# One encoder block on one core: the recurrent output projection made from seven combined products, and modulation rows moved between stages

## The chip, the cores and the metric

The kernel runs on one core of one Trainium2 chip. The metric is device time of one execution in microseconds (us); lower is better. The core has a matrix engine (TensorE, PE in the profile), three engines for elementwise work (VectorE or DVE, ScalarE or ACT, GpSimd or POOL), and SyncE (SP), whose queue issues nearly all DMAs here. Each engine works through its own list of instructions.

## The reference, cut to what matters

One layer of a hybrid encoder on x of 1024 tokens by 1024 channels, all in float32. The part that the change rewrites is the recurrent branch of the mixer.

```python
x = sandwich(x, ffn1, ..., 0.5)       # FFN 1
x = sandwich(x, mix,  ..., 1.0)       # mixer
x = sandwich(x, ffn2, ..., 0.5)       # FFN 2

mod = silu(c) @ w_ada + b_ada         # 9 rows of 1024: shift, scale, gate of each sub-layer

def mixer(h, ...):
    q, k, v, xr, yr, g_att, g_rec = split(h @ w_in)
    att = chunked_attention(q, k, v, rel_bias) @ w_att_o
    rec = (rg_lru(conv(xr), ...) * gelu(yr)) @ w_rec_o
    merged = sigmoid(g_att) * att + sigmoid(g_rec) * rec
    return merged @ w_out
```

## The kernel before, in words

**Numbers as two parts.** TensorE multiplies a rounded form of float32. So each operand X is cut into a high part (a CAST by ScalarE, L147) and a low part (X minus the high part, a subtraction by VectorE or GpSimd, L148), and each product is three matmuls: high by high, high by low, low by high. The helper `split` records both cuts, `prep` loads a weight tile into the pool of raw tiles (tag `raw`, three buffers) and cuts it, and `mm3` (L494 to L496) issues the three matmuls. A matmul has a 128x128 stationary operand and a moving one of 128x512.

**Stages, in order of time.** FFN 1, the recurrence with its input projections (`lru_phase`), the recurrent output (`rec_out_phase`), attention (`att_phase`), the merge of both branches (`merge_phase`), the output projection (`out_phase`), FFN 2. In FFN 1 and FFN 2 and in the output projection, 2x2 blocks of operands are already multiplied in seven combined products where eight would be the plain way: some products use sums of blocks of weights and of activations. An FFN's up half goes in 22 blocks of columns; blocks 4 to 21 of FFN 1 (3 to 21 of FFN 2) use seven products (L716 to L718), with the weight sums made by GpSimd one block ahead (`mix`, L694), and GpSimd also makes the sums for the down half (`all_sums`, L914). The down half is a list of units, one per product and pair of row blocks, each of 12 matmuls (L976).

**The recurrence.** For each of eight channel blocks b: projections, a convolution, two gates, then `scan`: ScalarE makes exponent, tanh, square and root (L1183 to L1187), GpSimd one product (L1189), VectorE the scan (L1190) and its product with the gelu branch (L1191, tile `a`). The result is cut at once into `rh` (ScalarE, L1193) and `rl` (VectorE, L1194).

**The recurrent output.** For each of eight channel blocks n: 48 matmuls make the gate (`gr` weights; ScalarE takes tanh, L1257), 48 matmuls make the output block (`ro` weights by `rh`, `rl`), VectorE multiplies both (L1269), and a DMA stores the block to `part` (L1270). Gate n+1 is placed ahead of output n. Two side tasks run beside this. `out_weights` loads `w_out`, makes the weight blocks and sums of the seven products of the output projection, cuts them (`wo`) and stores 28 tiles of 512 KB to `outw` in DRAM; the output projection loads them again (`wu`). And `bgq`, a queue of generators for modulation rows, is stepped by `bg`.

**Modulation rows.** `ada_acc` (L202 to L207) loads eight tiles of `w_ada` of 512 KB (`rawa`) and adds them up on VectorE with the weights `c_act`: one plain product and seven SCALAR_TENSOR_TENSOR on 128x1024. `ada_cols` turns the sum into columns (scale and shift), `ada_gate` into a gate row. Their number v is 3 for shift, 4 for scale and 5 for gate of the mixer, 6, 7 and 8 of FFN 2. Before, 2 (gate of FFN 1), 3 and 4 are worked off in FFN 1; 6, 7, 5 and 8 in the recurrent output. Gates 5 and 8 go to DRAM and are loaded later (`load_gate`). In the up half of FFN 1, hooks after products call first the constants of the recurrence (`early`), then `bg`: one hook per block, after product 3, with the `w_ada` tile in the temporary pool `u`. In the down half `bg` is called once per unit of the first three products.

**Order.** Inside FFNs, the output projection and (after the change) the new products, the order of each engine's instructions is as written (`manual_schedule`); elsewhere a scheduler orders them, and it may move later instructions of other generators in between. SP issues its DMAs in order; one that waits for a free buffer holds those behind it.

Of the kernel before, what the change touches and what calls it, by code (L numbers as in the profile page):

```python
# [23 lines left out]
P = 128  # L24
# [24 lines left out]
def kernel(  # L49
# [239 lines left out]
    gate_d = {sub: dpool.tile([P, D], F32, name=f"gate{sub}") for sub in (1, 2)}  # L289
# [224 lines left out]
    def ffn(sub, w_gu, w_down, hh, hl, xin, xout):  # L514
# [266 lines left out]
        def up_phase(started):  # L781
# [291 lines left out]

    C_Q, C_K, C_V, C_XR, C_YR, C_GA, C_GR = 0, 512, 1024, 1536, 2560, 3584, 4608
# [37 lines left out]

    def lru_phase(hh, hl, tail):
        rec_h, rec_l = [], []
# [64 lines left out]
        def scan(b, st):  # L1179
# [12 lines left out]
            rh, rl = t4("rh", F32R), t4("rl", F32R)  # L1192
            nc.scalar.copy(rh, a)  # L1193
            nc.vector.tensor_tensor(rl, a, rh.bitcast(F32), op=ALU.subtract)  # L1194
            rec_h.append(rh)
            rec_l.append(rl)
# [24 lines left out]
        def rest():  # L1221
            for kind, part in (("x", xr_part), ("y", yr_part)):
# [15 lines left out]
            return rec_h, rec_l, wts  # L1238
# [3 lines left out]
    def rec_specs():  # L1242
        specs = {}
        for n in range(KB + 1):
            if n < KB:
                specs["gr", n] = partial(prep_cols, w_in, C_GR + n * P)
            if n > 0:
                specs["ro", n - 1] = partial(prep_cols, w_rec_o[0], (n - 1) * P)
        for n in ("q", "k"):
            specs[n, 0] = partial(prep_cols, w_in, (C_Q if n == "q" else C_K))  # L1250
        return specs

    def rec_out_phase(hh, hl, rec_h, rec_l, wts, part, others):
        def gate(n):
            tg = tu("tg")
            for sh, pj in enumerate(proj(wts["gr", n], hh, hl)):
                nc.scalar.activation(tg[:, sh * 512 : (sh + 1) * 512], pj, AF.Tanh, scale=0.5)  # L1257
            return tg

        nxt = gate(0)  # L1260
        for n in range(KB):
            tg = nxt
            if n + 1 < KB:
                nxt = gate(n + 1)
            bg(4)
            pr = proj(wts["ro", n], rec_h, rec_l)
            for sh in range(2):
                sl = slice(sh * 512, (sh + 1) * 512)
                nc.vector.scalar_tensor_tensor(tg[:, sl], tg[:, sl], 1.0, pr[sh], op0=ALU.add, op1=ALU.mult)  # L1269
            nc.sync.dma_start(part[n * P : (n + 1) * P, :], tg)  # L1270
            for _ in range(4):
                bg()
                next(others, None)
        bg_flush()
        assert next(others, None) is None
# [285 lines left out]
    H1, H2 = slice(0, 512), slice(512, 1024)  # L1561

    def pair_steps(weights, top, bot):

        t1, t2, b1, b2 = top[:, H1], top[:, H2], bot[:, H1], bot[:, H2]
        add, sub_ = ALU.add, ALU.subtract
        if weights:
            return (t1, t2, t1, sub_), (t2, b2, t2, sub_), (b2, b2, t1, sub_), (b1, b1, b2, sub_)
        return (b2, t2, b2, add), (t2, t1, t2, sub_), (t1, b2, t1, sub_), (b1, b1, t1, sub_)

    OUT_PAIRS = KB // 2
    OUT_STREAM = (1, 2, 6, 5, 3, 7, 4)
    out_w = {
        (p, j): dpool.tile([P, 2, 512], F32, name=f"outw{p}_{j}") for p in OUT_STREAM for j in range(OUT_PAIRS)
# [555 lines left out]
```

## Time and profile before

| what | value |
|---|---|
| median of 3 runs | 2180.91 us (2178.07 to 2181.05) |
| the profiled execution | 2171.58 us |
| its span, first to last instruction | 2169.7 us |
| mean granted TensorE clock | 0.998 |
| matmul instructions | 9925 |
| recurrent output: first and last start of a matmul on `rh` | 912.4 and 1071.6 us |
| bytes moved by DMA | 383.55 MB |

Spans of instructions come from the profiled execution. A row of the timeline gives start, duration, engine, line of the kernel, operation, output and inputs, and in brackets how long the engine had been idle and what ended that. A row by groups gives the number of instructions, busy time and mean nanoseconds of one. A row by windows gives the busy time of PE, PEld, DVE, ACT and POOL in a stretch, each with its count, then the granted clock, the busy share of the DMA engines and GB/s.

### The profile page before, as it was taken

The page shows a single profiled execution, that of the slowest core. Times are in us where ns is not written, and L with a number is a line of the kernel's source. Part 1 is how long each engine was busy: PE and PEld are TensorE (multiplying, and loading weights), DVE is VectorE, ACT ScalarE, POOL GpSimd, SP SyncE. Part 2 cuts the span into 40 slices and gives each one's busy share as a digit, 9 for nine tenths or more (in the row PEclk, how much of TensorE's full clock was granted, in tenths as well). Part 3 has the DMA queues.
Part 4 walks back from the last instruction along what each step waited for, and adds up shares of the span by engine and source line. Part 5 has one row for each costly group of instructions (what it writes and reads, how often), then busy time and mean ns, then how long its engine had stood idle before and what let it go on. Part 6 is the DMA issues. An engine that isn't in the chain of part 4 may idle for free.

```text
span 2169.7 us, 26880 instructions
## 1 busy us (share of the span) xinstructions
PE 2130.5 (98%) x9925; PEld 1767.7 (81%) x9925; DVE 1335.1 (62%) x1796; ACT 1025.5 (47%) x1619; POOL 665.3 (31%) x498
## 2 busy tenths in 40 slices
PE   7999999999999999999999999999999999999998
PEld 5888788888878888888798988888888888888877
DVE  7755676567457777675436665576676564543466
ACT  5433333334447787722147777436443333334443
POOL 1168885431104011000021120002078883422102
PEclk9999999999999999999999999999999999999999
DMA  9356774368575111299812013467157653347365
GB/s 327 105 190 242 242 259 156 123 234 314 185 246 194 44 48 43 89 326 325 270 40 71 26 52 99 158 215 262 64 199 278 243 206 107 126 148 276 120 231 186
DMA packets 266364, 383.55 MB, mean 177 GB/s; under 512 B 17488, under 2 KB 171256, under 8 KB 266232
## 3 DMA queue, kind: packets, MB, share of 16 engines
q1 hardware_dynamic: 253312, 335.60, 46.3%
q10 hardware_dynamic: 12920, 46.23, 5.5%
q8 instruction: 78, 1.28, 0.2%
q14 instruction: 54, 0.44, 0.1%
HBM read 275.86 MB, written 109.05 MB: 177 GB/s over the span
## 4 chain that ended last, share of the span: by engine, by line
PE 82%; DVE 6%; DMA 6%; ACT 4%; issue 1%; SPq 1%; POOL 0%; POOLq 0%; DVEq 0%; ACTq 0%
PE px L976 8%; PE pv L976 7%; PE pj L494 7%; PE pj L495 7%; PE pj L496 7%; PE psX L716 6%; PE psX L718 6%; PE psX L717 6%; PE pj L1330 6%; PE psZ L716 3%; PE psZ L718 3%; PE psZ L717 3%; PE px L1667 2%; DMA rawd<-downs 2%; PE pv L1377 2%; PE pv L1667 2%
## 5 line engine op out<-in xcount | busy, mean ns | idle before, releaser
L147 ACT CAST dh<-rawd 128x1024 fp32r<-128x1024 f32 x154 | 161.1, 1053 | 207.2 <-PE pv L976 66.5
L148 DVE TENSOR_TENSOR dh<-rawd,dh 128x1024 fp32r<-128x1024 f32 x130 | 161.6, 1247 | 149.7 <-ACT dh L147 141.7
L707 DVE TENSOR_TENSOR wm<-raw,wm 128x512 fp32r<-128x512 f32 x152 | 159.9, 1055 | 151.1 <-ACT wm L706 145.9
L494 PE MATMUL pj<-hh,wh 128*128 128x512 f32 x562 | 221.1, 394 | 0.0
L495 PE MATMUL pj<-hl,wh 128*128 128x512 f32 x562 | 219.1, 390 | 1.1 <-DVE hl L357 1.1
L496 PE MATMUL pj<-hh,wl 128*128 128x512 f32 x562 | 219.1, 390 | 0.0
L976 PE MATMUL px<-dh,dh 128*128 128x512 f32 x608 | 187.5, 389 | 1.2 <-DVE dh L148 1.2
L976 PE MATMUL pv<-dh,dh 128*128 128x512 f32 x528 | 163.3, 390 | 3.3 <-DVE dh L148 3.3
L148 POOL TENSOR_TENSOR wl<-raw,wh 128x1024 fp32r<-128x1024 f32 x20 | 48.3, 2421 | 314.3 <-ACT wh L147 269.8
L976 PE MATMUL px<-dh 128*128 128x512 f32 x352 | 137.4, 390 | 0.0
L914 POOL TENSOR_TENSOR act<-act,act 128x512 f32<-128x512 f32 x54 | 85.4, 1582 | 168.3 <-DMA act<-act 109.8
L976 PEld LDWEIGHTS px<-dh,dh 128*128 128x128 f32 x608 | 113.9, 188 | 25.6 <-DVE dh L148 2.1
L495 PEld LDWEIGHTS pj<-hl,wh 128*128 128x128 f32 x562 | 105.6, 188 | 22.9 <-DVE hl L357 1.9
L496 PEld LDWEIGHTS pj<-hh,wl 128*128 128x128 f32 x562 | 105.5, 188 | 22.0
L494 PEld LDWEIGHTS pj<-hh,wh 128*128 128x128 f32 x562 | 105.5, 188 | 21.5 <-DVE a L529 0.3
L976 PEld LDWEIGHTS pv<-dh,dh 128*128 128x128 f32 x528 | 98.7, 188 | 25.6 <-DVE dh L148 5.5
L716 PE MATMUL psX<-hh,wm 128*128 128x512 f32 x296 | 115.4, 390 | 1.3 <-ACT mixes L739 1.1
L716 PE MATMUL psX<-hs,wm 128*128 128x512 f32 x296 | 115.6, 390 | 0.1
L717 PE MATMUL psX<-hl,wm 128*128 128x512 f32 x296 | 115.2, 389 | 0.0
L718 PE MATMUL psX<-hs,wm 128*128 128x512 f32 x296 | 115.2, 389 | 0.0
L717 PE MATMUL psX<-hs,wm 128*128 128x512 f32 x296 | 115.2, 389 | 0.0
L718 PE MATMUL psX<-hh,wm 128*128 128x512 f32 x296 | 115.1, 389 | 0.0
(345 smaller groups left out, 5487.0 us busy)
## 6 DMA issues: line engine op xcount, KB each, us to landing
rawa<-in_w_ada_dram SPq DMA_DIRECT2D x56, 512.0 KB, 5.5
rawd<-acts SPq DMA_DIRECT2D x88, 256.0 KB, 3.9
rawd<-downs SPq DMA_DIRECT2D x88, 256.0 KB, 4.4
raw<-in_w_in_dram SPq DMA_DIRECT2D x44, 512.0 KB, 3.7
raw<-in_ffn_w_gu_dram SPq DMA_DIRECT2D x43, 512.0 KB, 4.8
sr<-in_ffn_w_gu_dram SPq DMA_DIRECT2D x39, 512.0 KB, 6.0
act<-act SPq DMA_DIRECT2D x37, 512.0 KB, 5.0
acts<-act ACTq DMA_DIRECT2D x36, 512.0 KB, 4.1
```

The costliest lines, as they stand in the source:

```text
L147: nc.scalar.copy(hi, raw)
L148: (eng or nc.vector).tensor_tensor(lo, raw, hi.bitcast(F32), op=ALU.subtract)
L494: nc.tensor.matmul(dst, wh[:, kk, :], xhk[:, sl], start=first, stop=False)
L495: nc.tensor.matmul(dst, wh[:, kk, :], xlk[:, sl], start=False, stop=False)
L496: nc.tensor.matmul(dst, wl[:, kk, :], xhk[:, sl], start=False, stop=last)
L707: nc.vector.tensor_tensor(t[:, 1], src, t[:, 0].bitcast(F32), op=ALU.subtract)
L716: nc.tensor.matmul(dst, t[:, 0, kk, :], xh, start=first and kk == 0, stop=False, skip_group_check=True)
L717: nc.tensor.matmul(dst, t[:, 0, kk, :], xl, start=False, stop=False, skip_group_check=True)
L718: nc.tensor.matmul(dst, t[:, 1, kk, :], xh, start=False, stop=last and kk == 3, skip_group_check=True)
L976: nc.tensor.matmul(dst, a_[:, 0, tk], w_[:, 1, :], start=first and n == 0, stop=last and n == 2, skip_group_check=True,)
L1330: nc.tensor.matmul(d, a[:, k, :], b[k][:, sl], start=k == 0 and i == 0, stop=k == KB - 1 and i == 2)
L1667: nc.tensor.matmul(dst, a[:, s, tk], w[:, t, :], start=first and n == 0, stop=last and n == 2, skip_group_check=True)
```

## The change

**Seven products for the recurrent output.** The 1024x1024 product of `w_rec_o` (transposed) by the recurrent rows is done in 28 units: seven products p in the order 1, 2, 6, 5, 3, 7, 4, each over four pairs j of row blocks, 12 matmuls a unit. `RecOperands` holds the operands: `load` brings one raw weight tile of 128x512 per unit (from `w_rec_o` for p = 1, 2, 4, from a new DRAM tensor `recs` that holds sums for p = 6, 5, 3, 7), `cut` cuts weight and activation two units ahead, `sums` makes the activation sums in place. Results of 128x512 are copied and added into `ys`. The tiles `rh` and `rl` are gone: `a` is kept whole and cut unit by unit. `rec_sums` makes the sums of `w_rec_o` in float32 during the recurrence: per pair two loads, four subtractions or additions on VectorE, two stores.

**Gates.** Gates 0 and 1 come ahead of the 28 units, gates 2 to 7 behind them; the product with the gate is one instruction of 128x1024 (L1368 of the new kernel).

**Output projection.** `weight_sums` stores only products 3 to 7 (20 tiles); the blocks for products 1 and 2 are loaded plain from `w_out` at the end of the merge and cut there and in the output projection (`cut_w`).

**Modulation rows.** Rows 6 and 7 move to FFN 1, whose up half now has two hooks per block (after products 6 and 3), with the `w_ada` tile in the `raw` pool; row 8 moves to the down half of FFN 2 and no longer goes through DRAM; row 5 stays beside the recurrent output.

The diff, cut to its core:

```diff
@@ ada_acc
-            elif raw_home[0] == "u":
-                raw = tu("rawa")
@@ up_phase
-                    if i == 3:
+                    if i in (6, 3):
                         if next(early, BANK) is BANK and sub == 0:
-                            raw_home[0] = "u"
                             bg(1)
-                            raw_home[0] = "raw"
+    def rec_sums():
+        for j in range(OUT_PAIRS):
+            pair = [t4("rtop"), t4("rbot")]
+            rows = [slice((2 * j + i) * P, (2 * j + i + 1) * P) for i in range(2)]
+            for t, r in zip(pair, rows):
+                nc.sync.dma_start(t, w_rec_o[0, r, :])
+            yield
+            for o, a, b, op in pair_steps(False, *pair):
+                nc.vector.tensor_tensor(o, a, b, op=op)
+            for t, r in zip(pair, rows):
+                nc.sync.dma_start(rec_s[r, :], t)
+            yield
@@ scan
-            rh, rl = t4("rh", F32R), t4("rl", F32R)
-            nc.scalar.copy(rh, a)
-            nc.vector.tensor_tensor(rl, a, rh.bitcast(F32), op=ALU.subtract)
+            rec.append(a)
@@ rec_out_phase
+        gate(0, wts)
+        bg(2)
+        gate(1, wts)
+        bg(2)
+        ops.load(2)
...
+            ops.cut(2)
+            for p in OUT_STREAM:
+                if p in (1, 6, 7, 4):
+                    dst = chain
+                elif p != 3:
+                    dst = [bank("pv") for _ in range(half)]
+                for j in range(OUT_PAIRS):
+                    n = ops.order.index((p, j)) + 1
+                    ops.load(n + 3)
+                    for i in range(half):
+                        mm(dst[i], i, p, j, j == 0 and p in (1, 2, 5), j == OUT_PAIRS - 1)
+                    ops.cut(n + 2)
+                    if p == 1:
+                        ops.keep(3, j, t4("keep", F32R, (P, 2, 512)))
+                        ops.sums(j, 0)
+                    elif p == 2:
+                        ops.sums(j, 1)
+                    elif p == 4:
+                        next(others, None)
+                    elif j == 1:
+                        bg(1, False)
+                    if p == 7 and j < 2:
+                        gated(j)
@@ main
-        bgq.extend([ada_gate(0, 0.5), ada_cols(3), ada_cols(4)])
+        bgq.extend([ada_gate(0, 0.5)] + [ada_cols(v) for v in (3, 4, 6, 7)])
-        bgq.extend([ada_cols(6, 3), ada_cols(7, 3), ada_gate(1, 1.0, later=2), ada_gate(2, 0.5, later=2)])
+        bgq.append(ada_gate(1, 1.0, later=2))
-        load_gate(2)
+        bgq.append(ada_gate(2, 0.5))
```

What stands on the engines at the places that the prediction speaks of follows; numbers behind a name tell tiles apart.

First, VectorE where the recurrence ends, before: `q` is the scan of the last channel block, `a` its result, `acc` the sum of a modulation row, `wo` the weights for the output projection.

```order
L1186 SCALAR_TENSOR_TENSOR q_7085<-q_7085,tr_7062 128x1024
L1190 SCALAR_TENSOR_TENSOR q_7085<-a_7084,ti_7063 128x1024
L1191 TENSOR_TENSOR a_7084<-q_7085,g_7035 128x1024
L1194 TENSOR_TENSOR rl_7096<-a_7084,rh_7095 128x1024
L205 TENSOR_SCALAR acc_7219<-rawa_7220,c_act 128x1024
L207 SCALAR_TENSOR_TENSOR acc_7219<-rawa_7223,c_act,acc_7219 128x1024
L207 SCALAR_TENSOR_TENSOR acc_7219<-rawa_7226,c_act,acc_7219 128x1024
```

The same place after: the cuts of the first units (`wl` from `raw` is a unit's weight, `wh` from `a` its activation) stand behind the last scan.

```order
L1243 SCALAR_TENSOR_TENSOR q_7155<-q_7155,tr_7132 128x1024
L203 TENSOR_SCALAR acc_7226<-rawa_7227,c_act 128x1024
L205 SCALAR_TENSOR_TENSOR acc_7226<-rawa_7230,c_act,acc_7226 128x1024
L1247 SCALAR_TENSOR_TENSOR q_7155<-a_7154,ti_7133 128x1024
L205 SCALAR_TENSOR_TENSOR acc_7226<-rawa_7286,c_act,acc_7226 128x1024
L1248 TENSOR_TENSOR a_7154<-q_7155,g_7105 128x1024
L148 TENSOR_TENSOR wo_7299<-wbot_7296,wo_7299 128x512
L148 TENSOR_TENSOR wl_7309<-raw_7291,wl_7309 128x512
L148 TENSOR_TENSOR wh_7312<-a_5991,wh_7312 128x512
```

What moved: the cut of the recurrent rows went from inside the recurrence to behind its last scan, with two steps of a modulation row and one cut for the output projection in between.

Second, VectorE in the new list of units, around product 7 (there is no such place before). `ys` by `pv` are the additions behind product 3, `ys` by `px` those behind product 7; `tg` by `ys` are products with a gate; `wl` and `wh` are the cuts of units.

```order
L1385 TENSOR_TENSOR ys_7431<-ys_7431,pv_7619 128x512
L148 TENSOR_TENSOR wl_7800<-raw_7762,wl_7800 128x512
L148 TENSOR_TENSOR wh_7803<-a_6735,wh_7803 128x512
L1368 SCALAR_TENSOR_TENSOR tg_7173<-tg_7173,ys_7425 128x1024
L148 TENSOR_TENSOR wl_7822<-raw_7786,wl_7822 128x512
L148 TENSOR_TENSOR wh_7825<-a_7111,wh_7825 128x512
L205 SCALAR_TENSOR_TENSOR acc_7226<-rawa_7740,c_act,acc_7226 128x1024
L1368 SCALAR_TENSOR_TENSOR tg_7232<-tg_7232,ys_7427 128x1024
L148 TENSOR_TENSOR wl_7847<-raw_7808,wl_7847 128x512
L148 TENSOR_TENSOR wh_7850<-a_6176,wh_7850 128x512
L205 SCALAR_TENSOR_TENSOR acc_7226<-rawa_7829,c_act,acc_7226 128x1024
L148 TENSOR_TENSOR wl_7867<-raw_7833,wl_7867 128x512
```

Behind these come the `wh` of the same unit and the four additions on `px`. What is new: the additions, on which the last product waits, stand behind a step of the modulation row (`rawa_7829`) whose load is issued only after the first product with a gate has been stored.

Third, SP in the up half of FFN 1, one block, before: `raw` and `sr` are the two weight tiles of a block (gate and up columns).

```order
L544 DMA sr_2802<-in_ffn_w_gu_dram 128x8x128
L202 DMA rawa_2781<-in_w_ada_dram 128x1024
L544 DMA raw_3074<-in_ffn_w_gu_dram 128x8x128
L756 DMA act_145<-act_2662 128x1024
L544 DMA sr_2936<-in_ffn_w_gu_dram 128x8x128
```

And after, one block:

```order
L542 DMA sr_2838<-in_ffn_w_gu_dram 128x8x128
L200 DMA rawa_2817<-in_w_ada_dram 128x1024
L542 DMA raw_2836<-in_ffn_w_gu_dram 128x8x128
L200 DMA rawa_2900<-in_w_ada_dram 128x1024
L754 DMA act_137<-act_2695 128x1024
```

What moved: two `w_ada` tiles per block in place of one, and `raw` of a block is now issued behind its `sr` (`raw_2836` behind `sr_2838`). Before, it stood ahead: `sr_3076`, the partner of `raw_3074`, comes one block behind the last row shown.

More of the change, by code (lines that the diff above doesn't have):

```diff
@@ L287, in brow @@
         return bass.AP(tensor=src_row.tensor, offset=src_row.offset, ap=[[0, P], [1, D]])
-    gate_d = {sub: dpool.tile([P, D], F32, name=f"gate{sub}") for sub in (1, 2)}
+    gate_d = {1: dpool.tile([P, D], F32, name="gate1")}
     def load_gate(sub):
@@ L1111, in mixer_constants, with sum_store, weight_sums, emit @@
         yield
+    def sum_store(name, products):
+        return {
+            (p, j): dpool.tile([P, 2, 512], F32, name=f"{name}{p}_{j}") for p in products for j in range(OUT_PAIRS)
+        }
+    out_w = sum_store("outw", (3, 4, 5, 6, 7))
+    rec_s = dpool.tile([D, D], F32, name="recs")
+    def rec_sums():
[10 more added lines that the diff above has]
+            yield
+    def weight_sums(w, store):
+        def emit(p, j, src):
+            t = t4("wo", F32R, (P, 2, 512))
+            split(src, t[:, 0], t[:, 1])
+            nc.sync.dma_start(store[p, j], t.bitcast(F32))
+        def load(j):
+            pair = t4("wtop"), t4("wbot")
+            for i, t in enumerate(pair):
+                k = 2 * j + i
+                nc.sync.dma_start(t, w[k * P : (k + 1) * P, :])
+            return pair
+        ahead = load(0)
+        yield
+        for j in range(OUT_PAIRS):
+            top, bot = ahead
+            emit(3, j, bot[:, H2])
+            yield
+            for p, (o, a, b, op) in zip((5, 7, 6, 4), pair_steps(True, top, bot)):
+                if p == 6 and j + 1 < OUT_PAIRS:
+                    ahead = load(j + 1)
+                nc.vector.tensor_tensor(o, a, b, op=op)
+                emit(p, j, o)
+                yield
     def lru_phase(hh, hl, tail):
-        rec_h, rec_l = [], []
+        rec = []
         def gate_w(b):
@@ L1221, in rest @@
         def rest():
+            side = rec_sums()
             for kind, part in (("x", xr_part), ("y", yr_part)):
@@ L1237, in rest @@
                 scan(b, st[b])
-            return rec_h, rec_l, wts
+                next(side)
+            return rec, wts
         return SimpleNamespace(fetch=wts.fetch, head=head, rest=rest)
[L1242 to L1251, printed above, removed]
@@ L1253, in rec_out_phase, with gate_specs @@
[L1253 to L1272 removed]
+    def gate_specs(n0, n1):
+        return {("gr", n): partial(prep_cols, w_in, C_GR + n * P) for n in range(n0, n1)}
@@ L1273, in rec_out_phase @@
                 next(others, None)
         bg_flush()
-        assert next(others, None) is None
+        for _ in others:
+            pass
+        return wts
     def att_phase(hh, hl, wts0, tg_dram, n_ga):
@@ L1653, in merge_phase @@
             ops.cut((1, 2)[n % 2], n // 2)
-        ops.load(3)
+            if n == KB - 2:
+                ops.load(2)
+        ops.cut_w(2)
         return ops
@@ L1705, in product @@
             for j in range(OUT_PAIRS):
-                ops.load(ops.order.index((p, j)) + 5)
+                n = ops.order.index((p, j)) + 1
+                ops.load(n + (3 if p == 1 else 4))
                 for i in range(half):
                     mm(dst[i], i, p, j, first and j == 0, j == OUT_PAIRS - 1)
+                ops.cut_w(n + 2)
                 yield j
```

172 lines of the change are left out of this document (133 added, 39 removed).

## The prediction

> **What bounds the kernel now.** I read the page first, then TensorE's windows, its timeline, its waits, and last the rows of the places that the change touches. Busy times by engine, GpSimd's busy tenths and the granted clock in 40 slices of 54 us:
>
> ```profile
> PE 2130.5 (98%) x9925; PEld 1767.7 (81%) x9925; DVE 1335.1 (62%) x1796; ACT 1025.5 (47%) x1619; POOL 665.3 (31%) x498
> ...
> POOL 1168885431104011000021120002078883422102
> PEclk9999999999999999999999999999999999999999
> ```
>
> TensorE is busy 98% of the span at full granted clock; every other engine has room on average. So a matmul less is time less, at the pace at which matmuls follow each other, unless TensorE then waits for something else. The pace, from a stretch without a gap and from the timeline of FFN 1's down half (start, duration, engine, line, operation, count):
>
> ```profile
> 1400.00:1500.00 100.00, 100.00 (x443) 82.84 (x442) 67.27 (x97) 38.21 (x72) 6.65 (x10) 1.00 0.72 250
> ```
> ```profile
> 599.92 0.62 PE L976 MATMUL px<-dh,dh 128*128 128x512 f32 x2
> 600.38 0.39 PE L976 MATMUL px<-dh 128*128 128x512 f32 x1
> 600.60 0.62 PE L976 MATMUL px<-dh,dh 128*128 128x512 f32 x2
> ```
>
> 443 in 100 us are 0.226 each; three from 599.92 to 600.60 are 0.227 each. I take 0.227. A unit of 12 matmuls is then 2.72 us. What TensorE waited for (engine, line, releaser, total, times, longest), the rows that matter here out of the whole list:
>
> ```profile
> PE pv L976 <- DVE dh L148: 3.3, 5, 0.8
> ...
> PE pj L1330 <- DVE tg L1269: 2.0, 1, 2.0
> PE psZ L716 <- ACT pp L743: 1.8, 1, 1.8
> ...
> PE pg L314 <- DVE acch L148: 1.5, 1, 1.5
> PE psX L716 <- ACT mixes L739: 1.1, 1, 1.1
> ```
>
> In the recurrent output TensorE waits once, 1.5 us (`pg`, a modulation gate), and 2.0 us at its end (L1330). psZ and psX are in FFN 1's up half.
>
> **Term 1: matmuls.** The output projection of the recurrence, three matmuls of each kind:
>
> ```profile
> L494 PE MATMUL pj<-rh,wh 128*128 128x512 f32 x128 | 49.9, 390 | 0.0
> L496 PE MATMUL pj<-rh,wl 128*128 128x512 f32 x128 | 49.8, 389 | 0.0
> L495 PE MATMUL pj<-rl,wh 128*128 128x512 f32 x128 | 49.8, 389 | 0.0
> ```
>
> 3 x 128 = 384 go; 28 units x 12 = 336 come: 48 less, 48 x 0.227 = 10.9 us. These rows say 0.390 us for one, by which it would be 18.7; but starts are 0.227 apart, so 0.390 holds an overlap with the next. The Trainium skill, "Perfetto Trace Analysis", Identifying the Most-Contended Engine, says that busy time of matmuls is no good measure because they are pipelined; by their durations the forecast would be 7.8 us lower, and the starts in this trace agree with the page.
>
> **Term 2: the first unit.** The recurrent rows are no longer cut inside the recurrence, and VectorE makes the first cuts behind the last scan (first place shown above). The chain before:
>
> ```profile
> 890.66 1.06 ACT L147 CAST wh<-raw 128x1024 fp32r<-128x1024 f32 x1
> 894.83 1.05 ACT L1193 CAST rh<-a 128x1024 fp32r<-128x1024 f32 x1 [3.12 <-DVE a L1191]
> ```
> ```profile
> 909.84 2.29 DVE L1190 TENSOR_TENSOR_SCAN q<-a,ti 128x1024 f32<-128x1024 f32 x1 [4.66 <-POOL ti L1189]
> 912.17 1.23 DVE L1191 TENSOR_TENSOR a<-q,g 128x1024 f32<-128x1024 f32 x1
> ```
> ```profile
> L494 PE MATMUL pj<-rh,wh x128: 389/389/486, 912.4 to 1071.6; 128*128 128x512 f32 x128
> ```
>
> A step of a modulation row (one addition of 128x1024) in FFN 1, first with GpSimd at work, then without, and an `rl` cut of the same size:
>
> ```profile
> 478.75 2.32 DVE L207 SCALAR_TENSOR_TENSOR acc<-rawa,c_act,acc 128x1024 f32<-128x1024 f32 x1
> ...
> 487.70 1.27 DVE L207 SCALAR_TENSOR_TENSOR acc<-rawa,c_act,acc 128x1024 f32<-128x1024 f32 x1
> ```
> ```profile
> L1194 DVE TENSOR_TENSOR rl<-a,rh 128x1024 fp32r<-128x1024 f32 x8 | 9.8, 1219 | 1.2 <-ACT rh L1193 1.2
> ```
>
> TensorE comes to the first unit at 912.4. With the chain as it was, VectorE would then still have scan, one step, `a` and three cuts of 128x512 ahead (starts of such instructions in a row are some 0.1 closer than they are long, and half as many columns take 0.6, term 3): 909.84 + 2.2 + 1.2 + 1.1 + 1.8 = 916.1, a wait of 3.7. But the cast at 894.83, for which ScalarE idled 3.12 and which took 1.05, is gone, and all of the last block's tanh, exponent and root stood behind it: the scan can come 4.2 earlier, less up to 1.8 for three of the four sums of `w_rec_o` in the same queue. That is 911.9 to 913.7. I take a wait of 0.7; bounds 0 and 3.7.
>
> **Term 3: feeding the units.** Costs of a cut, and of float32 work back to back on VectorE while GpSimd is idle:
>
> ```profile
> L148 DVE TENSOR_TENSOR mo<-m,mo 128x512 fp32r<-128x512 f32 x28 | 18.3, 686 | 18.0 <-ACT mo L147 18.0
> ...
> L147 ACT CAST mo<-m 128x512 fp32r<-128x512 f32 x28 | 16.1, 618 | 25.4 <-DVE m L1651 25.4
> ```
> ```profile
> 1028.11 0.68 DVE L1594 TENSOR_TENSOR wtop<-wtop 128x512 f32<-128x512 f32 x1
> 1028.71 1.29 DVE L148 TENSOR_TENSOR wo<-wbot,wo 128x512 fp32r<-128x512 f32 x2
> ...
> 532.28 2.47 DVE L989 TENSOR_TENSOR yacc<-yacc,pv 128x512 f32<-128x512 f32 x4
> ```
>
> Back to back one takes 0.61. In product 1 a unit needs five on VectorE (two cuts, the kept cut for product 3, two sums): 3.05 against 2.72; in product 2 four, 2.44. So VectorE falls 0.33 x 4 = 1.3 behind and wins 1.1 back: I take 1.0, bounds 0 and 3. Behind product 2 stand four additions (2.47, last row) ahead of the cuts of the third unit of product 6; TensorE has two units, 5.4 us, ready, and VectorE comes to the additions about 3 us late: 1.4, bounds 0 and 2.8. ScalarE needs three casts of 0.62 per unit, 1.9, and does not bind.
>
> **Term 4: ahead of the last product.** At the second place shown, let product 3 end at 0. VectorE then does the last addition (0.8), two cuts (2.0), the gate (3.15), two cuts (4.4), a step (5.6), the gate (6.7), two cuts (7.9). The next step waits for a `w_ada` tile whose DMA stands on SP behind the store of the first gate's product, so it is issued between 3.9 and 5.7. Landing times (last column, median us from issue), and the spread for all `rawa`:
>
> ```profile
> rawa<-in_w_ada_dram SPq DMA_DIRECT2D x56, 512.0 KB, 5.5
> ...
> rawd<-downs SPq DMA_DIRECT2D x88, 256.0 KB, 4.4
> ...
> rawd<-in_ffn_w_down_dram SPq DMA_DIRECT2D x66, 256.0 KB, 5.5
> ...
> raw<-in_w_att_o_dram SPq DMA_DIRECT2D x8, 256.0 KB, 2.9
> ```
> ```profile
> DMA to landing us min/median/max: 3.2/6.0/8.4
> ```
>
> With 5.5 it lands at 9.4 to 11.2; step, two cuts and the first addition on `px` follow, 3.1 us, so the last product starts at 12.5 to 14.3 where TensorE is free at 10.9. With the fastest `rawa` load of this trace, 3.2, it is 10.9 (7.9 + 3.1 binds) to 12.0. I take 1.7, bounds 0 and 3.5.
>
> **Term 5: the waits of the stage before.** The `pg` wait (1.5) is gone, since the gate's sum is ready tens of us ahead of its matmul: -1.5. The 2.0 at the end stay: tanh of the last gate stands where L1269 stood.
>
> **Term 6: FFN 1's up half.** The psX and psZ waits (1.1 and 1.8) came from one jam: VectorE's constants of the recurrence, then GpSimd waiting for a late store.
>
> ```profile
> 238.74 0.16 DVE L1090 TENSOR_SCALAR sp_den<-sp_ee 128x8 f32<-128x8 f32 x1
> 244.97 0.16 DVE L1105 TENSOR_SCALAR sp_hx<-colsB 128x8 f32<-128x8 f32 x1
> ```
> ```profile
> 248.72 1.27 POOL L914 TENSOR_TENSOR act<-act,act 128x512 f32<-128x512 f32 x1 [6.14 <-DMA act<-act]
> ```
>
> With two hooks a block the same 6.4 us of constants come three blocks earlier, in a block behind which GpSimd has weights to sum, not the late `act`: 1.1 stays, 1.8 goes. Against it, 16 additions for rows 6 and 7 (of them about half here), and raw weights that land later (third place shown). I take 1.3 for that; net -0.5, bounds -3 and +8 (rival C).
>
> **Term 7: the rest.** FFN 1's third product now has a step per unit, FFN 2's first product the eight of row 8. Windows of FFN 1's products 2 and 6, and of FFN 2's product 1:
>
> ```profile
> 505.90:535.70 29.80, 29.80 (x136) 24.74 (x134) 26.19 (x21) 11.49 (x12) 4.80 (x2) 1.00 0.92 344
> 535.70:565.70 30.00, 30.00 (x140) 25.03 (x140) 11.48 (x12) 13.05 (x15) 2.41 (x1) 1.00 0.75 259
> ```
> ```profile
> 1933.00:1963.00 30.00, 30.00 (x134) 24.84 (x133) 13.78 (x13) 10.45 (x12) 6.30 (x4) 1.00 0.85 310
> ```
>
> Product 2 ran with steps, VectorE at 26.19 of 29.8 and DMA at 344 GB/s, and TensorE did not wait; product 6 has 18.5 us of VectorE free for 8 x 1.28 = 10.2, and FFN 2's product 1 16.2. The bytes are what is tight: 8 x 0.52 MB are 140 GB/s more on 259 or 310, so transfers fall behind by 5 to 9 us, against a lead of five units (13.6) less landing and cuts. I take 0.5, bounds 0 and 4. In the recurrence, 16 float32 operations (9.8 us) replace eight `rl` cuts of 1.22 (9.8), and TensorE never waited there: 0. The output projection gets eight cuts more, 4.9 us of VectorE beside its first product, with about 1 us to spare at the sixth and seventh unit: 0.2, bounds 0 and 3.
>
> **The sum.** -10.9 + 0.7 + 1.0 + 1.4 + 1.7 - 1.5 - 0.5 + 0.5 + 0.2 = -7.4. On the profiled execution's 2171.6 that is 2164.2. The median of the runs is 2180.9, 9.3 above it; I take the difference as the same for both kernels, so 2180.9 - 7.4 = 2173.5. About 0.2% (4.4 us) is what a measurement of this kernel can tell from no change.
>
> **The rivals.**
>
> A. The forecast, chance 0.56.
>
> B. The seams cost nothing: terms 2 to 4 at their lower ends, 2180.9 - 10.9 - 1.5 - 0.5 + 0.7 = 2168.7. For it: the similar seams in the FFNs cost 0.8 at most each (pv L976). Against: those have no steps and sums between additions and cuts. Chance 0.15.
>
> C. GpSimd in FFN 1 becomes the bound. It was nearly full while its own sums ran (the page's slices from 163 to 325 us, and this window), and VectorE and GpSimd slow each other (the two step rows of term 2):
>
> ```profile
> 250.00:270.00 20.00, 18.12 (x79) 14.31 (x78) 14.36 (x13) 6.75 (x12) 19.54 (x13) 1.00 0.78 286
> ```
>
> Two steps in each of six crowded blocks of 19 us (84 matmuls), each holding GpSimd about 1.05 (2.32 - 1.27), plus a raw tile that lands later (an estimate: by two issues and a step, 2 us), make a wait between psX's and psZ's, 1.3, in each block: 6 x 1.3 = 8 us; 2180.9 - 7.4 + 8 - 1.3 = 2180, no change. The Trainium skill, "SBUF — State Buffer", Who interferes with whom, says that a VectorE instruction with two SBUF inputs locks out a GpSimd instruction that reads SBUF for its whole length; by that rule a step would cost GpSimd 1.27 in place of the 1.05 that the rows show, and C would come out 12 x 0.22 = 2.6 later; the rows agree with the page in kind and lie a little under it. Chance 0.18.
>
> D. The raw ring sets the pace of the units: slower. Three raw buffers, one held all the time by a `w_ada` tile, leave two. A load can be issued only when the weight two units before is cut, so two units take landing + 0.62 + 0.69 + about 0.3 for issue. With 2.9 that is 2.26 a unit, under 2.72. With 4.4 it is 3.0 (28 x 0.28 = 8 us lost), with 5.5 it is 3.56 (28 x 0.84 = 23.5): 2180.9 - 7.4 + 23.5 - 4 (terms 3 and 4 overlap) = 2193. It decides from a landing of 4.6, where the 10.9 are eaten. For it: two of the three 256 KB rows are over 4 us. Against: these two are from FFNs, where the DMA share is 0.75 to 0.92 (the windows of term 7); here 0.26 MB per 2.72 us are some 100 GB/s. Chance 0.11.
>
> **How the numbers follow.** Range 2166 to 2183: B's lower side to C's upper, leaving out D and tails, under 2 in 10. Faster by over 0.2%: three quarters of A and all of B, 0.58. Within 0.2%: the rest of A and most of C, 0.29. Slower: D and C's tail, 0.13.
>
> **What would show it.** 48 matmuls less and 28 units in about 76 us plus 4 to 5 us of gaps, those at the third unit of product 6 and ahead of the last product, the latter behind an `acc` that waits for `rawa`; no `pg` wait; one jam of about 1 us near 180 in FFN 1. Wrong would be: gaps at every unit (D), psX or psZ waits in several blocks of FFN 1 (C), or a late first unit of about 4 us.

## The result, and the profile after

| | before | after |
|---|---|---|
| median of the runs, us | 2179.49 (2175.70 to 2181.05, 4 runs) | 2204.24 (2201.47 to 2205.69, 4 runs) |
| ratio, 95% interval | | 1.0115 [1.0097, 1.0133] |
| profiled execution, its span, us | 2171.6, 2169.7 | 2203.3, 2201.6 |
| first matmul of FFN 1's down half | 470.9 | 507.2 |
| first gate matmul of the recurrence | 732.9 | 770.3 |
| first matmul on the recurrent rows | 912.4 | 949.9 |
| first matmul of attention | 1074.4 | 1103.4 |

The change makes the kernel slower by 1.15%. The profiled execution of before was one of its fastest, so the spans differ by 31.9 and the medians by 24.7; stages are compared between the two profiles. Up to FFN 1's down half 36.3 are lost, up to the recurrent rows 1.2 more; the recurrent output wins back 8.5 (162.0 before, 153.5 after), and from attention to the end 2.9 are lost.

TensorE's waits after, over the whole program (releaser, total, times, longest):

```profile
PE psX L714 <- DVE pp L724: 13.7, 8, 2.3
PE psX L714 <- ACT mixes L737: 7.0, 3, 5.0
PE psZ L714 <- ACT pp L741: 4.5, 3, 2.1
PE px L1375 <- DVE ys L1385: 4.0, 1, 4.0
```

The first three are all in FFN 1's up half: 25.2 us where before had 2.9. The fourth is ahead of the last of the seven products. The up half in windows of 50 us, after (the figure behind POOL's is the granted clock):

```profile
150.00:200.00 50.00, 45.01 (x190) 36.40 (x189) 34.93 (x54) 15.40 (x28) 36.08 (x26) 0.93 0.66 231
200.00:250.00 50.00, 44.77 (x186) 35.57 (x185) 31.36 (x30) 14.21 (x25) 36.45 (x24) 0.96 0.69 236
250.00:300.00 50.00, 44.65 (x184) 34.87 (x183) 33.63 (x31) 15.59 (x28) 36.82 (x24) 0.97 0.74 251
```

and the third window before:

```profile
250.00:300.00 50.00, 48.12 (x211) 39.17 (x211) 34.39 (x34) 17.62 (x31) 47.02 (x31) 1.00 0.72 256
```

In this window no engine got fuller: GpSimd fell from 47.02 to 36.82 us, VectorE hardly moved, and 184 matmuls ran where 211 had. Whatever slowed the stage made everybody wait. The granted clock also fell, which it had not done before. A typical wait, on VectorE:

```profile
355.18 1.24 DVE L705 TENSOR_TENSOR wm<-raw,wm 128x512 fp32r<-128x512 f32 x1 [1.83 <-ACT wm L704]
356.34 2.31 DVE L205 SCALAR_TENSOR_TENSOR acc<-rawa,c_act,acc 128x1024 f32<-128x1024 f32 x1
358.58 1.75 DVE L705 TENSOR_TENSOR wm<-wsum,wm 128x512 fp32r<-128x512 f32 x1
360.25 0.68 DVE L724 TENSOR_TENSOR pp<-psX,pp 128x512 f32<-128x512 f32 x1
```

and on TensorE at that time:

```profile
358.34 0.39 PE L716 MATMUL psZ<-hh,wm 128*128 128x512 f32 x1
360.98 0.79 PE L714 MATMUL psX<-hs,wm 128*128 128x512 f32 x1 [2.26 <-DVE pp L724]
361.58 0.63 PE L715 MATMUL psX<-hs,wm 128*128 128x512 f32 x1
362.00 0.63 PE L716 MATMUL psX<-hs,wm 128*128 128x512 f32 x1
```

Product 4 goes on in the bank that `pp` has to read first. The hook after product 6 put a step (L205, 2.31 beside a busy GpSimd) between a weight cut that was itself late and the addition `pp`; the second cut takes 1.75 where 0.68 is its time alone. Behind the wait matmuls start 0.43 apart, not 0.227: half the clock. Who was late to begin with shows in the other engines' waits in the up half (120 to 480 us), after:

```profile
POOL sr L692 <- DMA raw<-in_ffn_w_gu_dram: 46.4, 7, 12.0
...
ACT wm L704 <- DMA raw<-in_ffn_w_gu_dram: 21.2, 9, 5.0
```

Neither line exists in the same view of before. These are the raw weights of the next block, which SP issues; SP's own waits there:

```profile
SPq L542 <- DVE wm L705: 69.2, 13, 9.9
SPq L200 <- DVE acc L205: 64.7, 11, 13.5
SPq L200 <- DVE wm L705: 37.8, 4, 19.2
```

L200 is the load of a `w_ada` tile: it stands on SP for 102 us in these rows until a raw buffer comes free, and the weights (L542) stand behind it or wait for a buffer themselves. (Before, the one load a block also stood on SP, 79 us for a buffer of pool u, and no raw weight was late.) The transfers themselves were no slower: a raw weight tile of this stretch landed 4.6 us after its issue in the median, and 4.8 before (`sr` 7.5 and 6.8). So the raw weights came late because they were issued late. The longest single wait (5.0 on `mixes`) is the constants of the recurrence, the first and last of 10.5 us of them on VectorE (6.4 before, counted from the same instruction), and the update behind them:

```profile
181.31 1.25 DVE L1099 TENSOR_SCALAR sp_den<-sp_ee 128x8 f32<-128x8 f32 x1
...
191.62 0.16 DVE L1114 TENSOR_SCALAR sp_hx<-colsB 128x8 f32<-128x8 f32 x1
191.69 0.68 DVE L724 TENSOR_TENSOR act<-act,psX 128x512 f32<-128x512 f32 x1
```

The 4.0 us ahead of the last product, on VectorE, after:

```profile
1017.10 0.68 DVE L148 TENSOR_TENSOR wh<-a,wh 128x512 fp32r<-128x512 f32 x1
1019.87 1.28 DVE L205 SCALAR_TENSOR_TENSOR acc<-rawa,c_act,acc 128x1024 f32<-128x1024 f32 x1 [2.09 <-DMA rawa<-in_w_ada_dram]
1021.12 0.69 DVE L148 TENSOR_TENSOR wl<-raw,wl 128x512 fp32r<-128x512 f32 x1
1021.73 0.68 DVE L148 TENSOR_TENSOR wh<-a,wh 128x512 fp32r<-128x512 f32 x1
1022.33 1.88 DVE L1385 TENSOR_TENSOR ys<-ys,px 128x512 f32<-128x512 f32 x3
```

### The profile page after: what moved, and what is told of

It is laid out like the page before. It is cut to its first block, busy times and chain, and to the rows that moved or that the text cites. A ratio compares the mean times of both kernels' runs of the same rounds, so it can differ in the third digit from the quotient of the medians.

```text
span 2201.6 us, 26980 instructions
## 1 busy us (share of the span) xinstructions
PE 2135.5 (97%) x9877; PEld 1764.5 (80%) x9877; DVE 1395.4 (63%) x1872; ACT 1046.8 (48%) x1675; POOL 669.3 (30%) x498
## 4 chain that ended last, share of the span: by engine, by line
PE 68%; DVE 12%; DMA 6%; ACT 6%; issue 4%; POOL 3%; SPq 0%; POOLq 0%; ACTq 0%; DVEq 0%
PE px L972 8%; PE pv L972 7%; PE pj L493 5%; PE pj L492 5%; PE pj L494 5%; PE pj L1512 5%; PE psX L714 4%; PE psX L716 4%; PE psX L715 4%; PE psZ L714 2%; PE psZ L715 2%; PE psZ L716 2%; DVE wm L705 2%; DMA rawd<-downs 2%; PE pv L1559 1%
## 5 line engine op out<-in xcount | busy, mean ns | idle before, releaser
L714 PE MATMUL psX<-hs,wm 128*128 128x512 f32 x296 | 117.6, 397 | 13.7 <-DVE pp L724 13.7
L704 ACT CAST wm<-raw 128x512 fp32r<-128x512 f32 x152 | 92.6, 613 | 70.2 <-POOL raw L692 49.0
L714 PE MATMUL psX<-hh,wm 128*128 128x512 f32 x296 | 116.8, 395 | 7.3 <-ACT mixes L737 7.0
```

The lines of the kernel that those rows point to most:

```text
L704: nc.scalar.copy(t[:, 0], src)
L714: nc.tensor.matmul(dst, t[:, 0, kk, :], xh, start=first and kk == 0, stop=False, skip_group_check=True)
```

## The experiments

Each ratio is to the kernel before, run beside it on the same chip, with its 95% interval. The last column is the first gate matmul of the recurrence in the profile: FFN 1's price is read there, against 732.9. Two profiles of the changed kernel gave 770.3 and 766.0, so differences of some 4 us in this column say little.

| kernel | ratio | FFN 1 ends, us |
|---|---|---|
| the change | 1.0115 [1.0097, 1.0133] | 770.3 |
| e4: rows moved, no products | 1.0153 [1.0137, 1.0168] | 768.6 |
| e5: products, FFN 1 as before | 1.0045 [1.0033, 1.0057] | 734.0 |
| e1: one hook | 1.0072 [1.0058, 1.0086] | 761.9 |
| e2: hooks after 3 and 4 | 1.0167 [1.0145, 1.0188] | 775.8 |
| e3: tile in pool u | 1.0092 [1.0078, 1.0107] | 765.2 |
| f1: loads, half of the additions | 1.0023 [1.0013, 1.0033] | 748.8 |
| f2: additions, no loads | 1.0031 [1.0019, 1.0043] | 750.0 |
| g3: constants after product 3 | 1.0066 [1.0053, 1.0080] | 759.7 |
| k1: tile in pool t4 | 1.0105 [1.0091, 1.0119] | 768.4 |
| k2: k1 and g3 | 1.0058 [1.0046, 1.0071] | 759.0 |
| k3: f2 and g3 | 1.0015 [1.0005, 1.0024] | 748.4 |
| g2: five waits filled | 1.0106 [1.0092, 1.0119] | 772.0 |
| h1: the change again | 1.0117 [1.0103, 1.0131] | 766.0 |
| h2: twelve waits filled | 1.0104 [1.0090, 1.0118] | 766.9 |
| e6: no steps between products | 1.0048 [1.0034, 1.0061] | 736.0 |
| g1: e6, rows 6 and 7 in the recurrence | 0.9976 [0.9967, 0.9985] | 733.5 |
| h3: g1, first six blocks only | 0.9989 [0.9980, 0.9998] | 735.4 |

**Which part of the change loses (e4, e5).** e4 puts the hooks, the raw pool and the rows' new places into the kernel before; e5 takes them out of the changed kernel.

```diff
# e4, on before: hooks, raw pool; rows 6, 7 to FFN 1; row 8 to FFN 2
+                    if i in (6, 3):
-                            raw_home[0] = "u"
+        bgq.extend([ada_gate(0, 0.5), ada_cols(3), ada_cols(4), ada_cols(6), ada_cols(7)])
# e5, on after: one hook, pool u; rows 6, 7 beside the gates
+                    if i == 3:
+                            raw_home[0] = "u"
-            bg(2)
+            bg(4)
```

> The kernel before with the moves of modulation rows alone: two hooks a block, raw pool, rows 6 and 7 in FFN 1, row 8 in FFN 2's down half; the recurrent output in the plain way. Theory: the whole loss comes from these moves; FFN 1's up half ends about 36 us later, FFN 2's down half costs 2, the wait for the gate (1.5) goes: 2179.5 + 33 = about 2212 (2204 to 2217). Rival: the loss needs the new products or the moved weight sums as well; then it is under 2190.

> The seven products with FFN 1 as it was before the change: one hook after product 3, pool u, rows 2 to 4; rows 6 and 7 go ahead of row 5 in the recurrent output, with four steps a gate behind the products instead of two. Theory: the whole loss of the change sits in FFN 1, so this is the time of before less what the products gain (8.4 us between the traces) plus 2.3 for row 8 in FFN 2: 6 us under the kernel before, ratio 0.996 to 0.998. Rival: rows 6 and 7 beside the gates make waits of their own there (a gate's bank, a row's end), the attention starts 3 us later or more and the ratio is 0.999 or over.

e4: 1.0153, 2208.6 us, in the range that its theory gave. The moves alone cost more than the whole change, and the products give 0.38 points (8 us, with an uncertainty of about 5) back. e5: FFN 1 ends at 734.0, so its loss is gone, but the kernel is still slower: the rival came true, in one place.

```profile
PE pg L313 <- ACT acch L147: 13.7, 1, 13.7
```

VectorE's last three additions of row 5 ahead of it:

```profile
1070.48 1.28 DVE L207 SCALAR_TENSOR_TENSOR acc<-rawa,c_act,acc 128x1024 f32<-128x1024 f32 x1 [0.70 <-DMA rawa<-in_w_ada_dram]
1075.49 1.28 DVE L207 SCALAR_TENSOR_TENSOR acc<-rawa,c_act,acc 128x1024 f32<-128x1024 f32 x1 [3.73 <-DMA rawa<-in_w_ada_dram]
1077.06 1.28 DVE L207 SCALAR_TENSOR_TENSOR acc<-rawa,c_act,acc 128x1024 f32<-128x1024 f32 x1 [0.28 <-DMA rawa<-in_w_ada_dram]
```

Three rows do not fit beside the shorter recurrent output: the end of the stage waits for tiles one by one.

**What in FFN 1 (e1, e2, e3).** All on the changed kernel:

```diff
-                    if i in (6, 3):
+                    if i == 3:              # e1
+                    if i in (3, 4):         # e2
+                            raw_home[0] = "u"   # e3, around bg(1)
```

> The changed kernel with the hook in FFN 1's up half after product 3 only, the w_ada tile still in the raw pool; the steps that no longer fit there run in the down half. Theory (place): the hook after product 6 puts a step on VectorE between a weight cut that waits for GpSimd and the addition pp on which product 4 waits; without it the 13.7 us of pp waits and the half clock behind them are gone, no more than 5 us of TensorE waits are left in the up half, the first matmul of the down half starts at 471 to 476 us (507.2 in the changed kernel, 470.9 before), and the time is about 2171 us (2168 to 2178), below the kernel before. Rival (ring): one w_ada tile per block still holds one of three raw buffers, so weights still land late; the waits for mixes and for psZ (7.0 and 4.5 us) stay and the time is about 2188. Rival (load): two steps a block are too much work beside GpSimd; half of the steps leave half of the loss, about 2187.

> The changed kernel with its two hooks a block after products 3 and 4 in place of 6 and 3: as many steps, loads and raw buffers in the up half, another place. Theory (place): no step stands ahead of pp any more, so the 13.7 us of pp waits and most of the half clock go; the constants of the recurrence still make one jam of 2 to 5 us; first matmul of the down half at 474 to 482, time 2173 to 2182. Rivals (ring, load): nothing they depend on has changed; waits of 20 us or more stay in the up half and the time is 2197 or more.

> The changed kernel with its two hooks, but the w_ada tile in the temporary pool u, as before the change: the raw ring is free for weights. Theory (place): the step still stands ahead of pp; 10 us or more of pp waits stay, the clock still drops, time 2193 to 2206. Rival (ring): weights land in time, the waits go by more than half, time 2190 or less.

e1: the `pp` waits are gone and the up half waits 7.3 us in all, more than the 5 expected. Its down half starts at 481.4, so most of the 36 us came back there, but the steps left over run at the end of the third down product, where TensorE waits once:

```profile
PE pc L221 <- DVE acc L205: 10.2, 1, 10.2
```

So its time, 22 us over what I expected, says little against the place; its profile also keeps GpSimd's waits for raw weights (37.2 us), as the ring theory wanted. e2 fell flat: no `pp` wait is left, but the step after product 4 now makes the copy `mixes` late, GpSimd's waits for raw weights grow to 64.6 us, and the time is worse, as the rivals had it:

```profile
PE psX L714 <- ACT mixes L737: 17.1, 8, 4.0
```

e3, in ScalarE's and GpSimd's waits in the up half:

```profile
ACT pp L743 <- DVE acc L207: 17.7, 5, 3.6
...
POOL act L914 <- DMA raw<-in_ffn_w_gu_dram: 2.0, 1, 2.0
```

The raw weights came in time again (2.0 in place of 46.4), although the `w_ada` loads stood on SP ahead of them for 99.7 us. But the tile took a buffer from `pp`, which lives in the same pool: TensorE then waited 15.4 us on psZ. My theory of the place alone had fallen; a step did harm wherever it stood, by its addition or by its buffer.

**Loads against additions (f1, f2), constants (g3), another pool (k1, k2, k3).**

```diff
+            elif not no_step[0]:            # f1: no addition from the hook after 6
+            elif no_load[0] and k:          # f2: no tile; the addition reads acc
+                raw = acc
-                    if i in (6, 3):
+                    if i == 3 or i == 6 and bg_on:   # g3: 6 only when the constants are done
+                            raw_home[0] = "t4"   # k1; k2 = k1 + g3; k3 = f2 + g3
```

> The changed kernel, its w_ada tiles loaded at both hooks as it does, but the addition at the hook after product 6 left out (so half of the additions of modulation rows in FFN 1's up half are missing from the result). So far: one hook (e1) took the pp waits away, another place (e2) turned them into waits for mixes, and the pool u (e3) into waits for pp by psZ. Theory (queue): VectorE's step of 2.3 us beside GpSimd, wherever it stands ahead of a result that TensorE waits for, is the wait, and the half clock comes on top; without the step behind product 6 the pp waits fall from 13.7 to under 3, the jam of the constants near 196 (5 us) stays, and the time is 2178 to 2188. Rival (ring): the loads into the raw ring make the weights late; they are all there, so more than 18 us of waits stay in the up half and the time is over 2196.

> The changed kernel with both hooks and all additions in FFN 1's up half, but with no w_ada tile loaded there except the first of a row: the addition reads its own sum instead (so the modulation rows come out as other numbers). Theory (queue): the pp waits stay at 10 us or more, the clock still drops, time 2192 to 2204; what goes is at most the waits for mixes and psZ that late weights make (e3 gave 8 us). Rival (ring): without the loads the up half runs with under 8 us of waits and the time is under 2184.

> The changed kernel with the constants of the recurrence at the hook after product 3 alone, as before the change, and the hook after product 6 used only once they are done. Theory: the jam near 196 us (5.15 us of waiting and about 3 us at half clock) comes from VectorE's constants at the hook after product 6, ahead of the results that product 7 waits for; at product 3 they cost 2 to 3.5 us as before the change, so the time falls by 3 to 6 us, to 2198 to 2201, and the pp waits stay. Rival: the jam moves with the constants and stays as long; no change, 2203 or more.

> The changed kernel with its two hooks, the w_ada tile in the large pool t4 (22 tiles): neither the raw ring nor the pool u is held. Theory (rings): GpSimd's waits for raw weights (46.4 us in the changed kernel, none before) are gone, as in f2, the first matmul of the down half comes at 482 to 488 (507.2 in the changed kernel), ratio to the kernel before 1.002 to 1.005. Rival (additions and bytes): the ring is not it; the waits for pp stay at 10 us or more and the ratio is 1.008 or over.

> k1 with the constants at the hook after product 3 alone, as in g3. Theory: ring and constants are most of the loss, and what is left is about 5 us of additions ahead of pp; down half from 471 to 479, and the seven products then show: ratio 0.996 to 1.000. Rival: the additions carry most; down half from 482 or later, ratio over 1.002.

> f2 (all additions in the up half, no w_ada tile loaded there but the first of each row, so the modulation rows come out as other numbers) with the constants at the hook after product 3 alone. Theory: within 3 us of k2, since with the tile out of the ring the loads cost nothing; down half from 471 to 479. Rival (bytes): loads delay weights even with a pool of their own; k3 is 5 us or more under k2.

f2: without the loads 0.85 points (18.5 us) come back, GpSimd's waits for raw weights are gone, and the `pp` waits fall by half, with every addition still in place. This was not the 2192 to 2204 of its theory; it took 2182.8, under the 2184 of the ring rival, though with 11.4 us of waits and not under 8:

```profile
PE psX L718 <- DVE pp L728: 6.9, 7, 2.2
PE psX L718 <- ACT mixes L741: 4.5, 1, 4.5
```

f1 came out as its theory said (product 4 no longer waits for `pp`, a jam of 4.7, 2180.8 us) and gives as much, 0.93 points, with its loads all issued. But it does not part the theories as I meant: a tile that no addition reads is also free as soon as it has landed, and GpSimd's waits for raw weights fell from 46.4 to 8.1. So the loss needs both, a load and an addition for which its tile is kept: taking either away brings most of it back, and the two gains are not to be added. g3 gives 0.50 points (11 us), more than the jam itself, and fewer `pp` waits. k1 missed: raw weights are no longer late, but the other half of each block's weights, `sr`, which is in t4, is (GpSimd's waits in the up half):

```profile
POOL wsum L692 <- DMA sr<-in_ffn_w_gu_dram: 43.9, 9, 13.2
```

k2 missed with it: its down half starts at 494.6, which its rival (additions) had asked for. k3 keeps all the additions, was to be within 3 us of k2 and is 11 under it, which its rival (bytes) had asked for. So the additions do not carry most of what k2 lost, and the bytes are not shown to be the cause either: f1 moves them all and stands at 1.0023, and the raw weights' transfers were no slower in the change. k3 does show the sum: loads and constants together are 1.0 of the 1.16 points (the mean of the change's two measurements). Taken singly they gave 0.85 and 0.50, so they share waits. In u and in t4 the tile saved 0.24 and 0.11 points, the second within the noise. Each time what else lives in its pool came late: raw weights in raw, `pp` in u, `sr` in t4. That, and e3's raw weights in time behind 99.7 us of standing loads, speaks for the buffer that the tile holds and against the queue that its load holds. It is not shown: a pool of its own for the tile was not tried.

**The clock (g2, h1, h2).** Idle matmuls with operands that are always there go ahead of products that waited:

```diff
+            idle(7)                 # also ahead of products 3 and 4
             run(7, chain, False)
+                fill = {(7, 7): 16, (8, 4): 8, (10, 3): 8, (12, 3): 8, (14, 4): 8}   # g2
```

> The changed kernel with idle matmuls (results unused) put at the five places in FFN 1's up half where its trace shows a long wait with a half clock behind it: 16 ahead of product 7 of block 7, 8 each ahead of product 4 of blocks 8 and 14 and of product 3 of blocks 10 and 12. They need no operand that is late, so they fill the wait. Theory (clock): the windows of the changed kernel lose about 10 us to the granted clock behind those waits; filled, the granted clock of these windows is 0.99 to 1.00 and the time falls by 5 to 10 us, to 2194 to 2199, though work is added and not one wait is shorter. Rival: the clock costs nothing beside the waits; the time is 2203 or more.

> The changed kernel itself, as the partner of h2 on the same chip. Both theories: a ratio to the kernel before of 1.010 to 1.014, as in its first runs, and a mean granted clock of 0.990 to 0.993.

> The changed kernel with idle matmuls (results unused) in twelve places of FFN 1's up half: the five of g2, and those of the other waits of its trace and of g2's, 4 to 8 matmuls each, 96 in all (96 x 0.227 = 21.8 us of work). Theory (clock): no wait of the up half is left that halves the clock, the mean granted clock rises to 0.996 or more, and the time is 5 to 10 us under that of h1, though 21.8 us of matmuls are added, since they lie in waits. Rival: the half clock costs little beside the waits; the time is within 3 us of h1, or above it.

In h2 the clock stayed full:

```profile
150.00:200.00 50.00, 48.59 (x212) 39.21 (x212) 32.69 (x55) 15.86 (x29) 35.12 (x25) 1.00 0.65 227
200.00:250.00 50.00, 47.41 (x203) 37.29 (x201) 33.60 (x30) 14.11 (x25) 37.55 (x25) 1.00 0.71 243
250.00:300.00 50.00, 48.79 (x210) 39.08 (x211) 35.85 (x33) 15.79 (x28) 37.67 (x25) 1.00 0.75 262
```

but its first down matmul stands at 502.6, h1's at 503.0, and the ratios overlap (h1 repeats the change at 1.0117; the medians are 2198.2 and 2200.4). So 96 matmuls, 21.8 us, and a full clock together moved the time by about 2 us, as the rival had it: TensorE did not set the pace of this stage, and its half clock was in the main a result of the waits, not a second loss. What the clock gained and what the matmuls cost were not measured apart. g2's forecast failed: behind other waits its clock still fell, to 0.93 and 0.97 in two of these windows, and its time tells nothing.

**The products by themselves (e6, g1, h3).**

```diff
-                    elif j == 1:                 # e6, on e5: no step between products
-                        bg(1, False)
+        bgq.extend([ada_cols(6), ada_cols(7)])   # g1, on e6: ahead of the recurrence
+                bg(2)                            # g1: behind each scan
+                bg(3 if b < 6 else 0)            # h3, in place of g1's
```

> As e5, without any step of a modulation row between the seven products (five a gate behind them instead of four). Theory: the 4.1 us ahead of the last product came from the step that stood ahead of its additions, so TensorE waits there under 0.5 us and the time is 4 to 6 us under that of e5. Rival: the additions are late without the step too, since VectorE has cuts and gates ahead of them; the wait stays over 2 us and the time is within 2 us of e5.

> As e6 (seven products without steps between them, FFN 1 as before the change), but rows 6 and 7 are stepped in the recurrence, two steps per channel block, and only row 5 beside the gates, three steps a gate. Theory: e5 and e6 lost what the products gained to one wait at the end of the gates (pg behind the last tile of row 5, 13.7 and 22.0 us), because a row goes as fast as one w_ada tile after the other lands; with 16 loads moved to the recurrence, where DMA is a quarter busy, that wait is under 2 us. Then FFN 1 is as before, the stage from the first unit to attention takes about 148 us (162.0 before), FFN 2 costs 2.3: 11 us under the kernel before, ratio 0.994 to 0.997. Rival: steps in the recurrence delay its scans or hold raw tiles of its weights, TensorE waits there 5 us or more, and the ratio is 0.998 or over.

> g1 with the steps of rows 6 and 7 in the first six channel blocks of the recurrence, three each, and none in the last two. Theory: g1's wait of 3.95 us ahead of the first unit comes from steps beside the last scan; it falls under 1.5 us and the time is 2 to 4 us under g1's, ratio to the kernel before 0.995 to 0.9975. Rival: the first unit waits for the scan and its cuts whatever stands beside it; the wait stays over 3 us and the ratio at g1's 0.9976.

e6: the wait ahead of the last product is gone, with only 1.3 us of waiting left in the 28 units (first start 915.6, last 993.3); its time does not show it, since the `pg` wait at the end grew to 22.0. g1 is faster than both kernels, 5.3 us under before by the medians, half of the 11 expected: attention starts at 1068.0, 6.4 earlier than before. It still waits 3.8 us ahead of its first unit, for this on VectorE:

```profile
912.16 1.22 DVE L1252 TENSOR_TENSOR a<-q,g 128x1024 f32<-128x1024 f32 x1
913.30 3.92 DVE L207 SCALAR_TENSOR_TENSOR acc<-rawa,c_act,acc 128x1024 f32<-128x1024 f32 x3
917.14 0.69 DVE L148 TENSOR_TENSOR wo<-wbot,wo 128x512 fp32r<-128x512 f32 x1
```

h3 took that wait away and paid more elsewhere: three steps a block made TensorE wait for the recurrence's gate weights (2.8, 1.6 and 2.8 us). Both halves of its expectation count: the mechanism held, the forecast of the time did not.

## Why the prediction was wrong

The forecast of 2173.5 was wrong in sign, by term 6; slower had been given 0.13. The terms, in order:

- **Term 1 (-10.9) held.** 336 matmuls at 0.227 are 76.3; e6 runs its units in 77.9 (915.6 to 993.3 and one matmul) with 1.3 of waits. In the changed kernel they took 85.7, with 6.6 of waits.
- **Term 2 (+0.7, bounds 0 to 3.7):** 0. In g1, with steps between the scan and the cuts, it came to 3.8, a little over the upper bound and for the reason given.
- **Term 3 (+1.0 and +1.4):** nothing in products 1 and 2; 1.3 at the third unit of product 6, as forecast. A wait of 1.3 between products 5 and 3, for ScalarE's copies, was not foreseen.
- **Term 4 (+1.7, bounds 0 to 3.5): the mechanism held, the size did not.** 4.0, behind an `acc` that waited for `rawa`. The load was issued at 1013.67 and landed 6.1 us later, not 5.5; e6 without the step has no such wait. The landing is only a part: in e5 this step waited 0.21 for its tile, and TensorE still waited 2.5 at this place. Behind the 4.0 the granted clock was 0.87 from 1023 to 1036, an estimated 1.7 more (13 x 0.13) that no term had.
- **Term 5:** the `pg` wait went; the 2.0 at the end became 1.4.
- **Left out:** rows 6 and 7 each end in 16 column matmuls that hold TensorE 1.7 us (979.57 to 981.27 before). They moved from the recurrent output to FFN 1: no change in the sum, but 3.4 of the 8.5 that the stage won are these, and 3.4 of FFN 1's loss. So it is in part luck that 8.5 is near the 7.6 of terms 1 to 5: in e4, with the rows moved and no new products, the stage takes 157.9, so by these traces the products are worth 4.4 of the 8.5 where terms 1 to 4 made 6.1.
- **Term 6 (-0.5, bounds -3 to +8) failed.** Three of its statements fell. First, "the same 6.4 us of constants come three blocks earlier, in a block behind which GpSimd has weights to sum, not the late `act`: 1.1 stays, 1.8 goes": they took 10.5 beside a GpSimd at work, and the wait behind them was 5.0; without them at that hook the kernel is 11 us faster (g3). Second, "raw weights that land later", priced at a part of 1.3: without the loads 18.5 us came back (f2), and about as much with the loads and without the addition after product 6 (f1). I had read in the order that two `w_ada` tiles a block stand on SP ahead of weights, and costed their landing, but not the buffer: each load waits for one (102 us in all) and then keeps it until its step. Third, the step itself was priced by its length and by what it takes from GpSimd (1.05 in rival C), not by what stands behind it: it comes ahead of `pp`, on which product 4 then waited 13.7 us in all; without that addition (f1) product 4 does not wait for `pp` at all.
- **Term 7:** FFN 2 and the output projection lost 2.9 where 0.7 was the sum. This was not tested further.

Rival C named the place and its sign, psX and psZ waits in several blocks, but the wrong mechanism: GpSimd did not become the bound, it idled for weights, and its price, 8 us, was about a fifth of the 36. Rival D had the right mechanism, a raw ring of which a `w_ada` tile holds a part, in the wrong stage: between the seven products the units were not paced by it. How much of what is left in k3 (15.5 us in FFN 1, of which 3.4 are the column matmuls and 5.7 more waits between products in the up half) is the additions, stays open.

## What to carry to other kernels

A side task is costed by what stands behind each of its instructions and by what else lives in the pool of its tiles: here raw weights, `pp` or `sr` came late as the tile was in raw, u or t4. Where an engine's stage average shows room, look for the one result in it on which the critical engine waits, and for what the hook would put ahead of that. Before pricing a second loss such as a lower clock, ask whether the engine sets the pace there: h2 put 21.8 us of matmuls into its waits, and the time did not grow.

## What the runs showed of the hardware

The granted clock fell to half behind short waits (matmuls 0.43 us apart in place of 0.227): of the six waits of 2.08 to 2.26 us in the changed kernel's up half four did it (such as the one at 360.98) and two did not; the shorter ones did not. The Trainium skill, "TensorE: Matmul & The Clock Gate", Part 1, speaks of an idle window of about 3.4 us; in these traces less was enough, so the measurement decides. And VectorE's work of the same form took longer while GpSimd was at work: a step 2.31 us (at 356.34) against 1.28 alone (at 1019.87), a cut 1.75 (at 358.58) against 0.68 (at 1021.73).
